# A decoder layer on one core: eighty TensorE transposes replaced by a layout exchange through DRAM

## The chip, the cores and the metric

The kernel runs on one core of a Trainium2 chip. A core has a matrix engine (TensorE, PE in the profile), a vector engine (DVE), a scalar engine (ACT), a general engine (POOL, hardly used here) and sixteen DMA engines that move data between DRAM, the on-chip memory (SBUF) and the accumulators (PSUM). DMA transfers are issued from queues; this kernel uses those of SP (weight loads) and of ACT (everything small). The metric is the device time of one execution in microseconds (us), median of several runs.

## The reference

```
h = rmsnorm(x, norm1_g)
z = h @ w_in                                  # 2048 -> 12824 columns
o_A, o_B, o_C, o_D = fox(z), conv(z), gla(z), pool(z)     # four mixers, 512 wide each
y = sum_n sigmoid(z_gate[n] + gate_b[n]) * (o_n @ w_branch[n])
x = x + y @ w_out
h2 = rmsnorm(x, norm2_g)
u = causal_dwconv(h2 @ ffn_up, ffn_dw, ffn_db);  a, v = split(u)
out = x + (silu(a) * v) @ ffn_down
```

Shapes: 256 tokens, width 2048, FFN width 5632 (a and v each), all float32.

## The kernel before

**Products.** Every product has 256 tokens on the output side, in two tiles of 128, and a quarter of 512 columns. The contraction runs over blocks of 128 rows. To keep float32 accuracy each operand is split into a high part in a reduced form and a rest: activations `xh`, `xl`, weights `wh`, `wl`. The generator `units` takes two contraction blocks at a time: SP loads raw weights `wr` (four blocks, 1 MB, three buffers), ACT casts them to `wh` (line 200), DVE subtracts to get `wl` (line 202); `wh` and `wl` have three buffers each. `product` then runs, for such a unit, eight matmuls with `wh` (lines 218 and 219) and four with `wl` (line 224). There are 545 units, nearly all of this size.

**Order.** Each engine works off its instructions in the order of the program. After a unit's matmuls `step` is called: it runs functions that were put down with `after(n, engine, f)` for this step, and those are placed on the engine behind the cast (A) or the subtraction (V) that was issued last. Because units are emitted three ahead of what TensorE does, what stands behind a cast stands ahead of the next one. Mixer work is emitted in small pieces between units by `pump`.

**Transposes.** An operand of a product must have its contraction rows on the partitions, while a result has tokens there. So results that become operands are turned. Before the change TensorE does it with 128x128 transposes against an identity into `pt`, eight for 256 tokens by 512 columns: `transposed_to` for the gate product of the convolution, the pooling input and the GLA queries and keys; `transposed` for the four quarters of y (line 268); a loop over the four quarters of the residual x (line 893). ACT and DVE copy or split `pt` afterwards.

**The FFN's exchange.** In the FFN the same turn is done without TensorE, in `half`. ACT puts the scaled result into `pu`, arranged by 32-row quarters. Four DMA transfers on ACT's queue (`mem<-pu`, 128 KB each, line 924) write it to a scratch tensor in DRAM, one fetch (`pw<-mem`, 512 KB, line 931) reads it back with quarters of rows and columns exchanged, and DVE turns each 32x32 block (STREAM_TRANSPOSE, line 937). The fetch comes six steps later, the turn nine. `pu` and `pw` have two buffers.

**Phases around the change.** First the convolution's two products and the pooling input; then gates and `branch` for each mixer, in the order 3, 1, 2, 0. In `branch(0)` each quarter of y is final: DVE multiplies the product by its gate (line 386), adds to y (387), and the quarter is transposed to `ah`, `al`. Then `w_out` takes four quarters of columns over y's four quarters of rows; each result is added to x (885), transposed, scaled into `h2h`, `h2l`, and squared for the norm (900). Then come FFN pairs.

Of the kernel before, what the change touches and what calls it, by code (L numbers as in the profile page):

```python
# [98 lines left out]
def layer(ctx, tc, a):  # L99
# [85 lines left out]
    def units(src, c0, n, sizes, loads, rows):  # L185

        k0 = have = 0
        loads = list(loads)
        for ks in sizes:
            if k0 == have:  # L190
                m = loads.pop(0)
                raw = wtile("wr", F32, m, n, LOAD, WR)
                nc.sync.dma_start(
                    out=raw,
                    in_=src[k0 * P : (k0 + m) * P, c0 : c0 + n].rearrange(rows, p=P),
                )
                base, have = k0, k0 + m
# [8 lines left out]
    def product(src, c0, n, stat, sizes=None, loads=None, tail=False, rows="(j p) n -> p j n"):  # L206

        nk = len(stat)
        acc = [accp.tile([P, 512], F32, name="acc") for _ in range(NT)]
        for k0, hi, lo in units(src, c0, n, sizes or [2] * (nk // 2), loads or [4] * (nk // 4), rows):  # L210
# [16 lines left out]
            step(1200.0)  # L227
        return acc

# [31 lines left out]
    def transposed(get, scales=None, tiles=None):  # L261

        hi, lo = tiles or act_tiles()
        for b in range(2):
            pt = tpp.tile([P, 2, S], F32, name="pt")
            for i in range(2):
                for t in range(NT):
                    T.transpose(pt[:, i, t * P : (t + 1) * P], get(t, 2 * b + i), ident)  # L268
            if scales is None:
                split_out(hi[:, 2 * b : 2 * b + 2], lo[:, 2 * b : 2 * b + 2], pt)  # L270
            else:
                for i in range(2):
                    split_out(hi[:, 2 * b + i], lo[:, 2 * b + i], pt[:, i], scales[2 * b + i])
        return hi, lo

# [3 lines left out]
    with ExitStack() as ph1:  # L279
        op_ = ph1.enter_context(tc.tile_pool(name="op", bufs=2))  # L280
        p1 = ph1.enter_context(tc.tile_pool(name="p1", bufs=1))
        gp = ph1.enter_context(tc.tile_pool(name="gp", bufs=5))
# [25 lines left out]
        def make_ssq(q):  # L308
            if q == 0:

                V.tensor_scalar(late, hT[3][1][:, 3, 0:1].bitcast(F32), 0.0, 0.0, ALU.max, ALU.min)
                A.activation(sqs, xts[q], AF.Square, bias=late)
            else:
                sq = gp.tile([P, 4, S], F32, name="gt")
                A.activation(sq, xts[q], AF.Square, bias=late)
                V.tensor_tensor(out=sqs, in0=sqs, in1=sq, op=ALU.add)
# [41 lines left out]
        def gates(n):  # L358
            out = []
            for d in range(4):  # L360
# [13 lines left out]
                out.append(g)  # L374
            return out

        def branch(n, g, oT, first=False, done=None):
            st = stationary([oT])
            for d in range(4):
                acc = product(w_branch[n], d * BW, BW, st)  # L380
                for t in range(NT):
# [3 lines left out]
                    else:  # L385
                        V.tensor_tensor(out=g[d][:, t], in0=acc[t], in1=g[d][:, t], op=ALU.mult)
                        V.tensor_tensor(out=yd, in0=yd, in1=g[d][:, t], op=ALU.add)
                if done is not None:
                    done(d)
# [85 lines left out]
        def logsig(pp, src, n, tag):  # L475

            e = pp.tile([P, n], F32, name=tag + "e")
# [5 lines left out]
        def gla_branch(pp, zc, gqT, gkT, tms, msk, wab, oT):  # L483
# [14 lines left out]
            e = logsig(pp, pl, 512, "gl")  # L498
# [8 lines left out]
            sr = pp.tile([P, NT, BW], F32, name="sr")  # L507
            A.activation(sr, zc[:, :, 528:1040], AF.Sigmoid)
            V.tensor_tensor(out=sr, in0=sr, in1=zc[:, :, 528:1040], op=ALU.mult)
            yield 1100  # L510
            go = pp.tile([P, NT, BW], F32, name="go")
# [117 lines left out]
        def fox_branch(pp, za, fb, sel, cb, msel, oT):  # L629
            rq = pp.tile([P, NT * 16], F32, name="fss")  # L630
            for t in range(NT):
                sq = pp.tile([P, 1024], F32, name="fsq")
# [32 lines left out]
            e = logsig(pp, lff, 16, "fl")  # L665
# [30 lines left out]
            fo = pp.tile([P, NT, BW], F32, name="fo")  # L696
# [69 lines left out]
        with tc.tile_pool(name="pDB", bufs=1) as pp:  # L766
# [9 lines left out]
            sg = gp.tile([P, NT, BW], F32, name="gt")  # L776
# [5 lines left out]
            later += [lambda q=q: make_ssq(q) for q in range(4)] + [make_rstd, gate_evac]  # L782
# [4 lines left out]
            nc.sync.dma_start(out=rc, in_=a["consts"][:, K_RC : K_RC + 64])  # L787
            for t in range(NT):
                V.scalar_tensor_tensor(
                    out=sg[:, t], in0=acca[t], scalar=rstd[:, t : t + 1], in1=sg[:, t],  # L790
                    op0=ALU.mult, op1=ALU.mult,
                )
            transposed_to(
                [lambda pt, b=b: A.copy(out=up[:, 2 * b : 2 * b + 2, CK - 1 :], in_=pt) for b in range(2)], sg
            )
            oB = o_tiles()
            later.append(lambda: bg.append(conv_branch(pp, up, oB)))
# [8 lines left out]
            zd = gp.tile([P, NT, BW], F32, name="gt")  # L806
            z_tok(zd, C_PZ, BW, BW)
            transposed_to(
                [lambda pt, b=b: A.copy(out=s0[:, 2 * b : 2 * b + 2, 16:], in_=pt) for b in range(2)], zd
            )  # L810
            oD = o_tiles()
            later.append(lambda: bg.insert(0, pool_branch(pp, pw, (s0, s1), oD)))
# [33 lines left out]
        with tc.tile_pool(name="pA", bufs=1) as pp:  # L846
# [5 lines left out]
            sst = pp.tile([P, 1024], F32, name="sst")  # L852
# [10 lines left out]
            g = gates(0)  # L863
            drain()
            yT = []
            branch(
                0, g, oA,
                done=lambda d: yT.append(
                    transposed(lambda t, i: y[:, t, (4 * d + i) * P : (4 * d + i + 1) * P])
                ),  # L870
            )
# [7 lines left out]
    h2S = []  # L879
    ss2 = p2.tile([P, NT, 4], F32, name="ss2")  # L880
    for d in range(4):
# [6 lines left out]
        for b in range(2):  # L888
            pt = tpp.tile([P, 2, S], F32, name="pt")
            for i in range(2):  # L890
                c = 4 * d + 2 * b + i
                for t in range(NT):
                    T.transpose(pt[:, i, t * P : (t + 1) * P], x2[:, t, c * P : (c + 1) * P], ident)  # L893
            for i in range(2):
                c = 4 * d + 2 * b + i
                split_out(hi[:, 2 * b + i], lo[:, 2 * b + i], pt[:, i], vec("n2", c))
        h2S += stationary([(hi, lo)])
        for t in range(NT):
# [3 lines left out]
            )  # L902
    s2 = p2.tile([P, NT], F32, name="s2s")
# [4 lines left out]
    up_ = ctx.enter_context(tc.tile_pool(name="fu", bufs=2))  # L908
    scr = ctx.enter_context(tc.tile_pool(name="scr", bufs=2, space=bass.MemoryType.DRAM))

    def half(pair, is_v, u):

        n = (NPAIR if is_v else 0) + pair
        acc = product(ffn_up, n * BW, BW, h2S)

        pu = up_.tile([P, 4, NT, P], F32, name="pu")
        for t in range(NT):
            A.activation(
                pu[:, :, t], acc[t].rearrange("p (q x) -> p q x", q=4), AF.Identity, scale=rstd2[:, t : t + 1]
            )  # L920

        mem = scr.tile([P, 4 * NT * P], F32, name="mem")
        for q in range(4):
            A.dma_start(
                out=mem[32 * q : 32 * q + 32].rearrange("r (k c) -> k r c", k=4),
# [110 lines left out]
```

## Time and profile before

| what | value |
|---|---|
| median of 3 runs | 1509.15 us (1508.7 to 1509.52) |
| profiled execution | 1508.69 us, span 1506.9 us |
| TensorE busy | 1501.5 us of the span |
| DVE busy | 997.9 us |
| ACT busy | 768.6 us |
| granted TensorE clock | 1.0 |

The span is the time from the first to the last instruction of the profiled execution; 1.8 us lie around it. An engine counts as busy only while it runs an instruction that computes; issuing a DMA counts as idle.

### The profile page before, as it was taken

How to read it: one execution, taken by the hardware profiler on the slowest of the kernel's cores; microseconds unless marked ns; L12 is line 12 of the kernel's file. 1: busy time of each engine (PE TensorE's matmuls, PEld its weight loads, DVE VectorE, ACT ScalarE, POOL GpSimd, SP SyncE). 2: the span in 40 equal slices, each digit the busy share in tenths (PEclk: the TensorE clock that was granted, in tenths of full speed). 3: DMA queues.
4: the chain of work that ended last, by engine and by line, in shares of the span. 5: the costliest groups of instructions: out<-in, count | busy, mean ns of one | idle time of the engine just before them, and what ended most of it. 6: DMA issues, size and time to landing. Idle time of an engine off the chain costs nothing.

```text
span 1506.9 us, 18227 instructions
## 1 busy us (share of the span) xinstructions
PE 1501.5 (100%) x7020; PEld 1259.6 (84%) x7020; DVE 997.9 (66%) x1272; ACT 768.6 (51%) x961; POOL 0.2 (0%) x4
## 2 busy tenths in 40 slices
PE   9999999999999999999999999999999999999998
PEld 8888889878998888888888888888888888888887
DVE  7799755666655656557555777764677745775775
ACT  7444365636456543444554655544555445544553
POOL 0000000000000000000000000000000000000000
PEclk9999999999999999999999999999999999999999
DMA  9656656545665466656556767765776657666774
GB/s 305 218 194 204 206 164 207 183 162 174 183 194 164 150 207 196 201 195 225 194 171 221 244 231 252 246 198 188 253 247 228 214 192 246 224 221 222 237 238 140
DMA packets 165450, 314.19 MB, mean 209 GB/s; under 512 B 6369, under 2 KB 32882, under 8 KB 164978
## 3 DMA queue, kind: packets, MB, share of 16 engines
q1 hardware_dynamic: 149680, 288.22, 58.3%
q10 hardware_dynamic: 15682, 24.81, 4.7%
q8 instruction: 55, 0.90, 0.2%
q14 instruction: 33, 0.27, 0.1%
HBM read 299.37 MB, written 13.63 MB: 208 GB/s over the span
## 4 chain that ended last, share of the span: by engine, by line
PE 99%; DMA 0%; DVE 0%; issue 0%; ACT 0%; ACTq 0%
PE acc L218 32%; PE acc L219 32%; PE acc L224 32%; PE mx L560 1%; DMA wr<-in_w_in 0%; PE mx L752 0%; PE mx L130 0%; PE mx L711 0%; PE pt L893 0%; PE pt L268 0%; PE mx L744 0%; PE pt L351 0%; PE mx L528 0%; PE mx L584 0%; PE mx L613 0%; PE mx L527 0%
## 5 line engine op out<-in xcount | busy, mean ns | idle before, releaser
L202 DVE TENSOR_TENSOR wl<-wr,wh 128x1024 fp32r<-128x1024 f32 (+4 forms) x545 | 646.4, 1189 | 422.6 <-ACT wh L200 420.1
L200 ACT CAST wh<-wr 128x1024 fp32r<-128x1024 f32 (+4 forms) x545 | 555.7, 1024 | 628.4 <-PE acc L219 548.7
L218 PE MATMUL acc<-wh,ah 128*128 128x512 f32 (+3 forms) x1344 | 514.2, 383 | 0.3 <-ACT wh L200 0.3
L219 PE MATMUL acc<-wh,al 128*128 128x512 f32 (+3 forms) x1344 | 511.9, 381 | 0.0
L224 PE MATMUL acc<-wl,ah 128*128 128x512 f32 (+3 forms) x1344 | 347.3, 380 | 0.0
L218 PEld LDWEIGHTS acc<-wh,ah 128*128 128x128 f32 x1344 | 252.7, 188 | 45.1 <-ACT wh L200 1.4
L219 PEld LDWEIGHTS acc<-wh,al 128*128 128x128 f32 x1344 | 252.7, 188 | 43.0 <-issue 0.6
L224 PEld LDWEIGHTS acc<-wl,ah 128*128 128x128 f32 x1344 | 249.1, 188 | 43.8
L219 PE MATMUL acc<-wh,h2l 128*128 128x512 f32 x704 | 274.0, 389 | 0.0
L218 PE MATMUL acc<-wh,h2h 128*128 128x512 f32 x704 | 273.9, 389 | 0.0
L224 PE MATMUL acc<-wl,h2h 128*128 128x512 f32 x704 | 188.2, 389 | 0.0
L219 PEld LDWEIGHTS acc<-wh,h2l 128*128 128x128 f32 x704 | 132.2, 188 | 27.4
L224 PEld LDWEIGHTS acc<-wl,h2h 128*128 128x128 f32 x704 | 132.1, 188 | 27.4
L218 PEld LDWEIGHTS acc<-wh,h2h 128*128 128x128 f32 x704 | 132.1, 188 | 27.3
L441 DVE SCALAR_TENSOR_TENSOR cacc<-up,vecT,cacc 128x256 f32<-128x256 f32 x120 | 51.0, 484 | 0.0
L218 PE MATMUL acc<-wh,oh 128*128 128x512 f32 x128 | 49.8, 389 | 0.0
L219 PE MATMUL acc<-wh,ol 128*128 128x512 f32 x128 | 49.8, 389 | 0.0
L937 DVE STREAM_TRANSPOSE zt<-pw 128x512 f32<-128x512 f32 x44 | 45.7, 1079 | 0.0
L953 ACT ACTIVATE ua<-ua 128x256 f32<-128x256 f32 x44 | 18.2, 414 | 48.8 <-issue 20.8
L948 DVE SCALAR_TENSOR_TENSOR uv<-zt,vecT,uv 128x255 f32<-128x255 f32 x88 | 41.7, 481 | 1.3
L948 DVE SCALAR_TENSOR_TENSOR ua<-zt,vecT,ua 128x255 f32<-128x255 f32 x88 | 41.3, 480 | 0.8
L983 DVE TENSOR_TENSOR x<-acc,x 128x512 f32<-128x512 f32 x40 | 25.8, 685 | 15.6 <-PE acc L224 15.6
(228 smaller groups left out, 641.5 us busy)
## 6 DMA issues: line engine op xcount, KB each, us to landing
wr<-in_ffn_up SPq DMA_DIRECT2D x88, 1024.0 KB
wr<-in_w_in SPq DMA_DIRECT2D x76, 1024.0 KB
wr<-in_ffn_down SPq DMA_DIRECT2D x44, 1024.0 KB
wr<-in_w_branch SPq DMA_DIRECT2D x16, 1024.0 KB
wr<-in_w_out SPq DMA_DIRECT2D x16, 1024.0 KB
wr<-in_w_in SPq DMA_DIRECT2D x16, 772.0 KB
mem<-pu ACTq DMA_DIRECT2D x88, 128.0 KB
pw<-mem ACTq DMA_DIRECT2D x22, 512.0 KB
```

The costliest lines, as they stand in the source:

```text
L200: mark["A"] = A.copy(out=hi, in_=part)
L202: mark["V"] = V.tensor_tensor(out=lo, in0=part, in1=hi.bitcast(F32), op=ALU.subtract)
L218: T.matmul(o, xh[:, s], hi[:, j], start=(k0 + j == 0), stop=False)
L219: T.matmul(o, xl[:, s], hi[:, j], start=False, stop=False)
L224: T.matmul(acc[t][:, :n], xh[:, s], lo[:, j], start=False, stop=(k0 + j == nk - 1))
L441: V.scalar_tensor_tensor(out=acc[:, c], in0=up[:, c, j : j + S], scalar=vec("cw", 4 * j + c), in1=acc[:, c], op0=ALU.mult, op1=ALU.add,)
L560: T.matmul(pss[h][:, q * P : (q + 1) * P], l_, r_, start=True, stop=True)
L937: V.transpose(out=zt[:, :, t * P : (t + 1) * P].rearrange("p j (k i) -> p j k i", k=4), in_=pw[:, :, t].rearrange("p k (i j) -> p j k i", ...
L948: V.scalar_tensor_tensor(out=u[:, c, sh:], in0=zt[:, c, : S - sh], scalar=vec("fw", tap * 88 + ch), in1=u[:, c, sh:], op0=ALU.mult, op1=AL ...
L953: A.activation(u[:, c], u[:, c], AF.Silu)
L983: V.tensor_tensor(out=x2[:, t, ds], in0=acc[t], in1=x2[:, t, ds], op=ALU.add)
```

## The change

The exchange of the FFN becomes a class `Exchange` that takes a tile pool, and is used for ten more turns: the gate product, the pooling input, the four quarters of y and the four of x. Their 80 TensorE transposes go; eight remain of those in `transposed_to` (GLA queries and keys). The turn reads contiguous blocks of four instead of a stride of four, so the weight columns of the FFN convolution and the rows of `ffn_down` change their order. The new pool `xq`, for the early exchanges and y, has one buffer; x uses the FFN's pool `fu`, which has two.

At two phase borders products run two at a time (`twin`): the first two quarters of `w_out` run over contraction blocks 0 to 7 each, then over 8 to 15, and the first FFN pair is cut at block 12. The gates of branch 0 are made in two halves, each followed by its two branch quarters.

```diff
+    def twin(src, c0s, n, stat, cut, done):
+        nk = len(stat)
+        accs = [acc_tiles() for _ in c0s]
+        for k0, k1 in ((0, cut), (cut, nk)):
+            for i, c0 in enumerate(c0s):
+                sizes = [2] * ((k1 - k0) // 2)
+                multiply(accs[i], n, stat, units(src, c0, n, sizes, [4] * ((k1 - k0) // 4), k0))
+                if k1 == nk:
+                    done(i, accs[i])
...
+    class Exchange:
+        def __init__(self, pool):
+            self.pool = pool
+            self.pu = pool.tile([P, 4, NT, 4, 32], F32, name="pu")
+        def put(self, t):
+            return self.pu[:, :, t].rearrange("p q j i -> p j q i")
+        def send(self):
+            self.mem = scr.tile([P, 4 * NT * P], F32, name="mem")
+            for q in range(4):
+                A.dma_start(
+                    out=self.mem[32 * q : 32 * q + 32].rearrange("r (k c) -> k r c", k=4),
+                    in_=self.pu[:, q].rearrange("p t j i -> p (t j i)"),
+                )
+        def fetch(self):
+            self.pw = self.pool.tile([P, 4, NT, 4, 32], F32, name="pw")
+            A.dma_start(out=self.pw.rearrange("p k t j i -> p (k t j i)"), in_=self.mem)
+        def turn(self, out):
+            for t in range(NT):
+                V.transpose(
+                    out=out[:, :, t * P : (t + 1) * P].rearrange("p j (k i) -> p j k i", k=4),
+                    in_=self.pw[:, :, t].rearrange("p k j i -> p j k i"),
+                )
+        def go(self, n_fetch, n_turn, out):
+            self.send()
+            after(n_fetch, "A", self.fetch)
+            after(n_turn, "V", lambda: self.turn(out))
+
+    xq = ctx.enter_context(tc.tile_pool(name="xq", bufs=1))
...
-                        V.tensor_tensor(out=yd, in0=yd, in1=g[d][:, t], op=ALU.add)
+                        if done is None:
+                            V.tensor_tensor(out=yd, in0=yd, in1=g[d][:, t], op=ALU.add)
+                        else:
+                            if t == 0:
+                                ex = Exchange(xq)
+                            V.tensor_tensor(out=ex.put(t), in0=cols(yd), in1=cols(g[d][:, t]), op=ALU.add)
...
-            g = gates(0)
+            g = gates(0, (0, 1))
             drain()
             yT = []
-            branch(
-                0, g, oA,
-                done=lambda d: yT.append(
-                    transposed(lambda t, i: y[:, t, (4 * d + i) * P : (4 * d + i + 1) * P])
-                ),
-            )
+            def y_done(ex):
+                hi, lo = act_tiles()
+                yT.append((hi, lo))
+                yt = xq.tile([P, 4, S], F32, name="yt")
+                ex.go(6, 8, yt)
+                after(9, "V", lambda: split_out(hi, lo, yt))
+            branch(0, g, oA, done=y_done)
+            branch(0, gates(0, (2, 3)), oA, done=y_done)
...
     nc.sync.dma_start(out=x2, in_=a["x"][0].rearrange("(t p) d -> p t d", p=P))
     yS = stationary(yT)
-    h2S = []
+    up_ = ctx.enter_context(tc.tile_pool(name="fu", bufs=2))
+    h2 = []
     ss2 = p2.tile([P, NT, 4], F32, name="ss2")
-    for d in range(4):
-        acc = product(w_out, d * BW, BW, yS)
+
+    def out_done(d, acc):
+        ex = Exchange(up_)
         for t in range(NT):
             xd = x2[:, t, d * BW : (d + 1) * BW]
             V.tensor_tensor(out=xd, in0=acc[t], in1=xd, op=ALU.add)
+            A.copy(out=ex.put(t), in_=cols(xd))
         hi = hp.tile([P, 4, S], F32R, name="h2h", tag="h2h")
         lo = hp.tile([P, 4, S], F32R, name="h2l", tag="h2l")
-        for b in range(2):
-            pt = tpp.tile([P, 2, S], F32, name="pt")
-            for i in range(2):
-                c = 4 * d + 2 * b + i
-                for t in range(NT):
-                    T.transpose(pt[:, i, t * P : (t + 1) * P], x2[:, t, c * P : (c + 1) * P], ident)
-            for i in range(2):
-                c = 4 * d + 2 * b + i
-                split_out(hi[:, 2 * b + i], lo[:, 2 * b + i], pt[:, i], vec("n2", c))
-        h2S += stationary([(hi, lo)])
+        h2.append((hi, lo))
+        xt = up_.tile([P, 4, S], F32, name="zt", bufs=1)
+        ex.go(6, 8, xt)
+        def scaled():
+            for i in range(4):
+                split_out(hi[:, i], lo[:, i], xt[:, i], vec("n2", 4 * d + i))
+        after(9, "V", scaled)
         for t in range(NT):
             sq = p2.tile([P, BW], F32, name="sq2", bufs=2)
             A.activation(
                 sq, x2[:, t, d * BW : (d + 1) * BW], AF.Square, accum_out=ss2[:, t, d : d + 1]
             )
+
+    twin(w_out, (0, BW), BW, yS, 8, out_done)
+    for d in (2, 3):
+        out_done(d, product(w_out, d * BW, BW, yS))
```

Not shown: the same replacement for the gate product and the pooling input (`ex.go(6, 8, ...)` each, and one more multiplication of the gate on ACT), the FFN's use of the class with (6, 9), the twin call for the first FFN pair with cut 12, and tiles that are reused to make room (`gp` has four buffers instead of five).

**DVE at the last two quarters of y (d2 and d3 of branch 0), before.** `gt<-acc,gt` is the gate multiply, `y<-y,gt` the final sum, `al<-pt,ah` the split of a transposed half.

```order
L386 TENSOR_TENSOR gt<-acc,gt 128x512 x2
L387 TENSOR_TENSOR y<-y,gt 128x512 x2
L202 TENSOR_TENSOR wl<-wr,wh 128x1024
L248 TENSOR_TENSOR al<-pt,ah 128x512 x2
L202 TENSOR_TENSOR wl<-wr,wh 128x1024
```

The same engine and place after the change; `pu<-y,gt` is the sum, written into the exchange's layout, and `yt<-pw` the turns.

```order
L434 TENSOR_TENSOR gt<-acc,gt 128x512 x2
L440 TENSOR_TENSOR pu<-y,gt 128x4x4x32 x2
L202 TENSOR_TENSOR wl<-wr,wh 128x1024 x2
L434 TENSOR_TENSOR gt<-acc,gt 128x512 x2
L440 TENSOR_TENSOR pu<-y,gt 128x4x4x32 x2
L202 TENSOR_TENSOR wl<-wr,wh 128x1024 x4
L280 STREAM_TRANSPOSE yt<-pw 128x4x128 x2
L202 TENSOR_TENSOR wl<-wr,wh 128x1024
L310 TENSOR_TENSOR al<-yt,ah 128x1024
L202 TENSOR_TENSOR wl<-wr,wh 128x1024
L280 STREAM_TRANSPOSE yt<-pw 128x4x128 x2
```

The split stood one subtraction behind the sum; now four subtractions and the turns lie between the last put and the first split, and the second put stands two subtractions behind the first.

**ACT at the same place, after the change.** `mem<-pu` are the four sends of a quarter, `pw<-mem` the fetch; before, this engine had here only casts and pairs of `L247 CAST ah<-pt 128x512`.

```order
L200 CAST wh<-wr 128x1024 x3
L268 DMA mem<-pu 4x32x256 x4
L200 CAST wh<-wr 128x1024 x2
L268 DMA mem<-pu 4x32x256 x4
L275 DMA pw<-mem 128x1024
L200 CAST wh<-wr 128x1024 x3
L275 DMA pw<-mem 128x1024
L309 CAST ah<-yt 128x1024
L200 CAST wh<-wr 128x1024 x2
L309 CAST ah<-yt 128x1024
```

The fetch of the first of the two quarters now stands directly behind the sends of the second.

**ACT at the last quarter of x, before.** `sq` are the squares, `h2h<-pt` scaled casts of transposed quarters, `x2r` the square root for the norm.

```order
L250 ACTIVATE h2h<-pt,vecT 128x256 x2
L200 CAST wh<-wr 128x1024
L250 ACTIVATE h2h<-pt,vecT 128x256 x2
L235 ACT_TABLE_LOAD
L235 ACTIVATE x2r<-x2v 128x2
L200 CAST wh<-wr 128x1024 x7
```

The same place after the change:

```order
L941 COPY pu<-x_5559 128x4x4x32
L955 ACTIVATE sq_6221,ss_5564<-x_5559 128x512
L941 COPY pu<-x_5559 128x4x4x32
L955 ACTIVATE sq_6223,ss_5564<-x_5559 128x512
L268 DMA mem<-pu 4x32x256 x4
L297 ACT_TABLE_LOAD
L297 ACTIVATE x2r<-x2v 128x2
L200 CAST wh<-wr 128x1024 x3
L275 DMA pw<-mem 128x1024
L200 CAST wh<-wr 128x1024 x3
L312 ACTIVATE h2h<-zt,vecT 128x256 x4
```

Two copies and four sends came in ahead of the next cast; the scaled casts moved six casts back.

## Rows read from the trace of the kernel before

**Rows 1.** The profile page: span, busy time of each engine, chain of waits.

```profile
span 1506.9 us, 18227 instructions
...
PE 1501.5 (100%) x7020; PEld 1259.6 (84%) x7020; DVE 997.9 (66%) x1272; ACT 768.6 (51%) x961; POOL 0.2 (0%) x4
...
PE 99%; DMA 0%; DVE 0%; issue 0%; ACT 0%; ACTq 0%
```

**Rows 2.** Timeline of TensorE, starts of units: start us, duration, line, operation.

```profile
665.17 0.39 PE L218 MATMUL acc<-wh,ah 128*128 128x512 f32 x1
...
667.89 0.39 PE L218 MATMUL acc<-wh,oh 128*128 128x512 f32 x1
...
673.34 0.39 PE L218 MATMUL acc<-wh,oh 128*128 128x512 f32 x1
...
677.03 0.39 PE L218 MATMUL acc<-wh,oh 128*128 128x512 f32 x1
...
715.36 0.39 PE L218 MATMUL acc<-wh,ah 128*128 128x512 f32 x1
...
719.10 0.39 PE L218 MATMUL acc<-wh,ah 128*128 128x512 f32 x1
```

**Rows 3.** Groups on TensorE: busy us, mean ns of one, idle time before.

```profile
L893 PE MATMUL pt<-ident,x 128*128 128x128 f32 x32 | 5.0, 280 | 0.0
L268 PE MATMUL pt<-ident,y 128*128 128x128 f32 x32 | 5.0, 279 | 0.0
...
L351 PE MATMUL pt<-ident,gt 128*128 128x128 f32 x24 | 3.6, 272 | 0.0
```

**Rows 4.** Timeline of ACT and DVE in a steady stretch, idle before in brackets.

```profile
659.03 1.05 ACT L200 CAST wh<-wr 128x1024 fp32r<-128x1024 f32 x1 [1.67 <-PE acc L219]
...
660.12 1.23 DVE L202 TENSOR_TENSOR wl<-wr,wh 128x1024 fp32r<-128x1024 f32 x1 [1.50 <-ACT wh L200]
```

**Rows 5.** Timeline of ACT in the FFN: put, sends, casts, fetch.

```profile
808.05 2.35 ACTq L924 DMA_DIRECT2D mem<-pu  x4
810.50 2.00 ACT L200 CAST wh<-wr 128x1024 fp32r<-128x1024 f32 x2 [2.48 <-issue]
...
816.35 0.35 ACTq L931 DMA_DIRECT2D pw<-mem  x1
```

**Rows 6.** DMA activity from 852 to 861 us in forty slices: tenths busy, GB/s.

```profile
DMA  9999999624222222222222222229974999999999
GB/s 382 437 419 410 391 400 401 228 50 109 91 91 77 68 82 87 91 96 100 82 77 77 96 91 96 96 96 191 205 100 155 264 341 337 355 419 423 423 369 400
```

**Rows 7.** DMA queues from 1317.4 to 1322.6 us, from the fetch's issue on.

```profile
q10 hardware_dynamic: 143, 0.52, 25.7%
```

**Rows 8.** Groups by form on DVE and ACT: busy us, mean ns of one.

```profile
L937 DVE STREAM_TRANSPOSE zt<-pw 128x512 f32<-128x512 f32 x44 | 45.7, 1079 | 0.0
...
L386 DVE TENSOR_TENSOR gt<-acc,gt 128x512 f32<-128x512 f32 x24 | 15.5, 686 | 7.4 <-PE acc L224 7.4
...
L250 ACT ACTIVATE h2h<-pt,vecT 128x256 fp32r<-128x256 f32 x16 | 6.7, 469 | 0.0
...
L235 ACT ACT_TABLE_LOAD x4 | 5.1, 1283 | 0.1
L900 ACT ACTIVATE sq<-x 128x512 f32<-128x512 f32 x8 | 5.0, 625 | 1.4 <-DVE x L885 1.4
```

**Rows 9.** Timeline of ACT's queue: two of three loads of constants.

```profile
201.43 0.35 ACTq L819 DMA_DIRECT2D gx<-in_consts  x1
...
202.29 0.53 ACTq L826 DMA_DIRECT2D wab<-in_gla_ba  x1
```

**Rows 10.** DMA packets from 203 to 204.9 us, all of ACT's queue.

```profile
DMA packets 77, 0.63 MB, mean 332 GB/s; under 512 B 0, under 2 KB 0, under 8 KB 0
```

**Rows 11.** Timeline of SP's queue: the load of the residual x.

```profile
696.04 0.37 SPq L877 DMA_DIRECT2D x<-in_x  x1
```

**Rows 12.** DMA queues from 697 to 703 us; the last column is the share.

```profile
q1 hardware_dynamic: 300, 2.14, 99.5%
```

More of the change, by code (lines that the diff above doesn't have):

```diff
@@ L183, in wtile, with units @@
         return w[:, : ks * BW].rearrange("p (j n) -> p j n", j=ks)[:, :, :n]
-    def units(src, c0, n, sizes, loads, rows):
-        k0 = have = 0
+    def units(src, c0, n, sizes, loads, k0=0):
+        have = k0
         loads = list(loads)
@@ L204, in units, with multiply @@
             k0 += ks
-    def product(src, c0, n, stat, sizes=None, loads=None, tail=False, rows="(j p) n -> p j n"):
+    def multiply(acc, n, stat, groups, tail=False):
         nk = len(stat)
-        acc = [accp.tile([P, 512], F32, name="acc") for _ in range(NT)]
-        for k0, hi, lo in units(src, c0, n, sizes or [2] * (nk // 2), loads or [4] * (nk // 4), rows):
+        for k0, hi, lo in groups:
             ks = hi.shape[1]
@@ L227, in product, with acc_tiles, cols @@
             step(1200.0)
-        return acc
+    def acc_tiles():
+        return [accp.tile([P, 512], F32, name="acc") for _ in range(NT)]
+    def product(src, c0, n, stat, sizes=None, loads=None, tail=False):
+        nk = len(stat)
+        acc = acc_tiles()
+        multiply(acc, n, stat, units(src, c0, n, sizes or [2] * (nk // 2), loads or [4] * (nk // 4)), tail)
+        return acc
+    def twin(src, c0s, n, stat, cut, done):
+        nk = len(stat)
+        accs = [acc_tiles() for _ in c0s]
[5 more added lines that the diff above has]
+                    done(i, accs[i])
+    scr = ctx.enter_context(tc.tile_pool(name="scr", bufs=2, space=bass.MemoryType.DRAM))
+    def cols(ap):
+        return ap.rearrange("p (j q i) -> p j q i", q=4, i=32)
+    class Exchange:
[25 more added lines that the diff above has]
+    xq = ctx.enter_context(tc.tile_pool(name="xq", bufs=1))
     def rsqrt(pool, ssq, n, scale, tag):
@@ L356, in transposed_to, with gates @@
             later.extend([None, lambda: half(0), lambda: half(1)])
-        def gates(n):
-            out = []
-            for d in range(4):
+        def gates(n, ds=range(4)):
+            out = {}
+            for d in ds:
                 bias = gp.tile([P, BW], F32, name="gb", tag="gb", bufs=3)
@@ L378, in branch @@
             st = stationary([oT])
-            for d in range(4):
+            for d in g:
                 acc = product(w_branch[n], d * BW, BW, st)
@@ L805, in layer @@
             V.memset(pool_tmp[:, 0:16], 0.0)
[L806 to L810, printed above, removed]
+            ex = Exchange(xq)
+            acc = product(w_in, C_PZ, BW, hS)
+            for t in range(NT):
+                A.activation(ex.put(t), cols(acc[t]), AF.Identity, scale=rstd[:, t : t + 1])
+            ex.go(6, 8, s0[:, :, 16:])
             oD = o_tiles()
-            later.append(lambda: bg.insert(0, pool_branch(pp, pw, (s0, s1), oD)))
+            after(8, "V", lambda: bg.insert(0, pool_branch(pp, pw, (s0, s1), oD)))
             g = gates(3)
@@ L905, in layer, with half @@
     rstd2 = rsqrt(p2, s2, NT, 1.0 / D, "x2")
[L908 to L911 removed]
+    def half(pair, is_v, u, acc):
         n = (NPAIR if is_v else 0) + pair
[L914 to L916 removed]
+        ex = Exchange(up_)
         for t in range(NT):
[L918 to L925, printed above, removed]
[L926 to L940 removed]
+            A.activation(ex.put(t), cols(acc[t]), AF.Identity, scale=rstd2[:, t : t + 1])
+        zt = up_.tile([P, 4, S], F32, name="zt", bufs=1)
         def conv(c):
@@ L953, in conv @@
                 A.activation(u[:, c], u[:, c], AF.Silu)
-        after(6, "A", fetch)
-        after(9, "V", turn)
+        ex.go(6, 9, zt)
         for c in range(4):
@@ L963, in pair_up @@
         hi, lo = act_tiles()
-        half(pair, False, ua)
-        half(pair, True, uv)
+        us = (ua, uv)
+        c0s = [(is_v * NPAIR + pair) * BW for is_v in range(2)]
+        if pair == 0:
+            twin(ffn_up, c0s, BW, h2S, 12, lambda i, acc: half(pair, i, us[i], acc))
+        else:
+            for i in range(2):
+                half(pair, i, us[i], product(ffn_up, c0s[i], BW, h2S))
         def glu():
@@ L980, in down @@
             ds = slice(d * BW, (d + 1) * BW)
-            acc = product(w, d * BW, BW, st, tail=last and d == 3, rows="(p j) n -> p j n")
+            acc = product(w, d * BW, BW, st, tail=last and d == 3)
             for t in range(NT):
```

79 lines of the change are left out of this document (25 added, 54 removed).

## Prediction

> **What bounds the kernel now.** The page comes first: TensorE is busy 1501.5 of 1506.9 us, and the chain of waits is 99% PE [rows 1]. So the time falls only by what TensorE no longer does, and rises by any wait put in its way. Next the timeline of TensorE: a "unit" (8 products with wh, then 4 with wl) starts at 665.17 and the next at 667.89, 2.72 us on. At a border with transposes a unit lasts longer: 673.34 to 677.03 in the stage of y, 715.36 to 719.10 in that of x [rows 2].
>
> The groups of TensorE give what those transposes cost by their number: 32 for y, 32 for x, 24 in the helper of the first phase [rows 3]. Their busy times (5.0, 5.0, 3.6) overlap other matmuls; the unit lengths tell the truth.
>
> Then the engines that feed TensorE. Each unit needs a cast on ACT (1.05 us) and a subtraction on DVE (1.22 us). In a steady stretch ACT starts the cast at 659.03 and ends it near 660.1, DVE subtracts from 660.12 to 661.35 [rows 4], and TensorE starts that unit at 665.17, since three buffers stand between them. So wh is 5.1 us ahead. wl is first read after 8 of the 12 products, 8/12 x 2.72 = 1.8 us into the unit, so it is 5.6 us ahead. **This lead is what any new work queued ahead of a cast or a subtraction may eat; what exceeds it stalls TensorE.**
>
> **What the change removes.** 80 transposes in ten groups of 8: four quarters of y, four of x, the gate product and the pooling input. A unit with a group of 8 costs 3.69 - 2.72 = 0.97 us more in y, 3.74 - 2.72 = 1.02 in x [rows 2]. The two early groups have no row of their own here; at the same 0.97 each, 10 groups give **-9.9 us**. Nothing hides this: TensorE has no other idle time.
>
> **What it adds.** Each group becomes an exchange: a put into pu, four sends to DRAM, a fetch into pw, two turns on DVE. No engine work lands on TensorE, so each costs nothing until it overruns the lead. The FFN already does this, and gives prices. ACT issues four sends from 808.05 in 2.35 us, and its fetch, which waits for all four, issues at 816.35: 8.3 us until pu is free and the data is in DRAM [rows 5]. The sends run at some 90 GB/s in the tail of the window, at two tenths of the DMA engines [rows 6]. The fetch's 0.52 MB are through 5.2 us after its issue, with loads beside them [rows 7]; I take 5. A turn pair is 2 x 1.08 us, the gate multiply and the put 0.69 us for each half [rows 8].
>
> **The y borders.** Let 0 be the start of w_branch quarter d3 (or d1), units 2.72 apart; d2 has just ended. DVE multiplies and puts d2 until 3.1, ACT ends the third cast ahead at 3.1 and sends. xq has one buffer, so pu is free at 3.1 + 8.3 = 11.4. The product of d3 ends at 5.4 and its put could run from 6.8, but must wait: it ends at 11.4 + 1.4 = 12.8. Queued behind it on DVE is the subtraction of the unit that starts at 10.9: it ends at 14.0, TensorE wants it at 10.9 + 1.8 = 12.7. Stall 1.3 us, at both borders. Without the wait this put costs nothing.
>
> Next, the sends of d3 issue from 12.8 and the fetch of d2 right behind them at 15.4, on the same queue. If the fetch is independent it lands at 20.4. If its packets go behind the sends', it lands when these have (12.8 + 8.3 = 21.1) plus 1.3 for its 0.52 MB at some 400 GB/s [rows 6], at 22.4. The trace favours the latter: a load of constants was issued at 201.43, and two small ones behind it by 202.29 + 0.53 [rows 9], yet from 203 to 204.9 the queue moved 77 packets, none under 8 KB [rows 10]. [...] The turn and the subtraction behind it (2.1 + 1.2) must end by 21.8 + 1.3 + 1.8 = 24.9, so the fetch must land by 21.6: 0 or 0.8 us of stall. First border: 1.3 + 0.8 = **2.1**.
>
> At the second border the residual x (2.1 MB) is loaded on the SP queue. Its place is memory that y held, so it waits for the put of d3 and issues at the same 12.8 as the sends. Before, it was issued at 696.04 [rows 11] and ran alone, 2.14 MB in 6.0 us at 99.5% of all sixteen engines [rows 12]. How it shares engines with the sends no row shows. Lower bound: no harm, 0.8 us. Upper bound: its 6.0 us go ahead of the sends, the fetch lands at 28.4, stall 6.8. The nearest rows lie on both sides (weight loads just before and after sends leave them their 90 GB/s [rows 6]; the load of x takes every engine [rows 12]), so I take the middle, **3.8**.
>
> Two more steps follow here alone, because w_out reads d2 and d3 soon: the cast of ah queues ahead of wh (0.3 us), and the fetch of d3 waits for the turn of d2, pw being single. From the end of that turn 5 + 2.1 + 1.2 = 8.3 us pass to the subtraction that TensorE wants after 1.2 + 5.4 = 6.7: 1.6, less the 0.3 already lost, 1.3. Second border: 1.3 + 3.8 + 0.3 + 1.3 = **6.7**. y together 8.8, bounds 3.1 (no order, no harm) to 11.8.
>
> **The x borders.** Here pu and pw are double. Per quarter ACT has two copies (as long as a square, 0.63), two squares and the sends (2.35), after two adds on DVE (1.4) [rows 8, 5]. From the end of the product: sends from 3.5, ended 5.8, the cast behind them done 6.9; TensorE wants it at 8.2. So d0 is free. Its fetch holds ACT until 3.5 + 8.3 = 11.8; a cast later, at 13.2, ACT can take up d1, its twin, which ended at 10.9. Sends from 15.8, the cast behind them done at 19.2, wanted at 10.9 + 8.2 = 19.1: the lead is used up. The fetch of d1 holds ACT until 15.8 + 8.3 = 24.1; then come four scaled casts (4 x 0.47), three casts, and four scaled casts that wait for the turns, to 33.6. DVE, behind the same turns, adds d2 (ended 32.6) only from 36; ACT's sends end at 41.8, the next cast at 42.8, wanted at 40.8. That is 1.9 late if nothing gives way, 0 from a clean start; halfway, 0.9. d3 has a table load and a root (1.5) between its sends and the next cast: 6.9 + 1.5 = 8.4 for 8.2, and DVE's adds come up to 2.5 late again, as one subtraction and four splits (1.2 + 4 x 0.48) stand ahead of them: 0.2 to 2.7. d2's backlog is certain to last in part, so I take 2.1. Sum **3.0**, bounds 0.2 and 4.7.
>
> **Small edits.** The early exchanges: the turns come eight units after the put and the engines have over 1.7 us of lead left; the conv and pooling start later, but are fillers whose results are wanted many units on. 0, at most 1. The two-at-a-time FFN pair moves two evacuations closer: 0 to 1.5, I take 0, since its leads come out at 1.3 and 1.9. The other row order of ffn_down and of the weight columns, the reused tiles: same bytes and counts, 0.
>
> **Sum** against the profiled execution: 1508.69 - 9.9 + 8.8 + 3.0 = **1510.6 us**. That execution lies 0.46 under the median of the runs, inside their spread.
>
> **Rivals.**
> - *The load of x goes wholly ahead of the sends* (slower). Place: the second y border. Price: S = 6.8 instead of 3.8, so 1513.6; it decides once that stall passes 4.9 us. For it: the load takes every engine [rows 12]. Against: sends lost little next to weight loads [rows 6]. [...]
> - *The fetch does not wait for the sends behind which it is queued*, and x does no harm. Both borders 1.3, the second 0.5 for pw: y 3.1, so 1508.69 - 9.9 + 3.1 + 3.0 = 1504.9. For it: sends take two tenths of the engines, most are free [rows 6]. Against: [rows 9, 10].
> - *The leads absorb nearly everything*: puts are not held because sends land sooner than the fetch's issue suggests (8.3 is when ACT came to it), and x starts clean. Then 1499 to 1501. For it: ACT waits 1.67 us for TensorE in every steady unit [rows 4]. Against: four sends alone already hold an FFN cast back by 2.48 us [rows 5], and one pu cannot be refilled before it is read.
>
> **Numbers.** A measurement of this kernel tells 0.2% (3.0 us) from no change. Forecast 0.35, rival one 0.25, two 0.25, three 0.15. Faster: three, and half of two, with a little of the forecast's lower side (0.30). Slower: most of rival one and of the forecast's upper side (0.30). Same: the rest, 0.40. The range leaves out three and what exceeds the upper bounds: 1503.5 to 1515.5.
>
> **What would show it.** Right: no transposes at the borders, TensorE gaps of about 1 us two units after each y border ended by DVE; the put of d1 and d3 waiting on mem<-pu for some 4 us; turns of d2 waiting on the fetch; the cast after x's sends ending the waits of TensorE. Wrong: units at 2.72 us straight through the borders (rival three), or one gap of over 5 us at the load of x (rival one). What would make it wrong altogether is a stall where I put none, in the twin pair of the FFN or in the early phase.

## The result and the profile after

The changed kernel takes 1525.49 us (median of 4 runs, 1524.68 to 1528.14) against 1509.04 before: ratio 1.0112, interval 1.0094 to 1.0129. It is slower by 16.5 us, where 1.9 us were forecast. Its profiled execution took 1525.28 us.

The page of the changed kernel:

```profile
span 1523.5 us, 18152 instructions
...
PE 1500.5 (98%) x6940; PEld 1256.7 (82%) x6940; DVE 992.6 (65%) x1288; ACT 765.4 (50%) x963; POOL 0.2 (0%) x4
...
PEclk9999999999999999998999999999999999999999
...
PE 86%; DVE 5%; DMA 4%; ACT 2%; issue 2%; ACTq 1%; SPq 0%; DVEq 0%
```

TensorE runs 80 products fewer than in [rows 1] (6940 against 7020), but it is no longer nearly the whole chain of waits (86% against 99%), and one slice in the middle has less than nine tenths of the granted clock. So the saving is there, and more than that was lost to waits. The waits of all engines in groups (engine and line that waited, what released it: us in all, times, longest) name them:

```profile
ACT wh L200 <- DMA wr<-in_w_out: 16.3, 1, 16.3
...
DVE pu L440 <- DMA mem<-pu: 13.0, 2, 6.5
...
DVE yt L280 <- DMA pw<-mem: 10.2, 2, 6.5
PE acc L217 <- ACT wh L200: 9.8, 5, 4.7
...
PE acc L223 <- DVE wl L202: 7.1, 3, 2.8
```

The two middle lines are the y borders: DVE waits 13.0 us in two places for the sends to free pu, and 10.2 us for fetches. The last two are what TensorE paid itself.

Where it was paid is read from single units, which take 2.72 us undisturbed [rows 2]. Each window here runs from one unit's start to the next one's, with the busy time of each engine, then the granted clock:

```profile
core 0: us, PE busy (x) PEld busy (x) DVE busy (x) ACT busy (x) POOL busy (x), PEclk, DMA share, GB/s
64.39:68.53 4.14, 2.89 (x13) 2.07 (x11) 0.02 (x1) 1.09 (x2) 0.00 (x0) 1.00 0.42 142
640.79:647.08 6.29, 3.48 (x14) 2.49 (x12) 3.56 (x4) 0.00 (x0) 0.00 (x0) 0.92 0.16 52
647.08:650.93 3.85, 3.85 (x14) 3.08 (x12) 2.36 (x2) 2.73 (x3) 0.00 (x0) 0.69 0.87 259
656.37:660.81 4.44, 3.00 (x13) 2.18 (x12) 3.06 (x4) 1.73 (x2) 0.00 (x0) 1.00 0.45 148
701.62:707.45 5.83, 3.02 (x14) 2.18 (x13) 3.53 (x4) 0.00 (x0) 0.00 (x0) 1.00 0.33 84
707.45:716.62 9.17, 4.49 (x14) 3.24 (x12) 0.06 (x2) 1.10 (x2) 0.00 (x0) 0.69 0.89 339
716.62:721.55 4.93, 4.93 (x13) 3.92 (x14) 2.34 (x2) 1.84 (x2) 0.00 (x0) 0.54 0.62 209
800.77:805.59 4.82, 2.88 (x14) 2.07 (x12) 1.15 (x8) 3.11 (x7) 0.00 (x0) 1.00 0.59 222
805.59:810.03 4.44, 4.44 (x12) 3.54 (x13) 3.48 (x4) 2.58 (x3) 0.00 (x0) 0.62 0.61 195
869.89:874.46 4.57, 2.89 (x14) 2.07 (x12) 3.76 (x9) 2.50 (x5) 0.00 (x0) 1.00 0.66 242
```

Length less 2.72: 1.4 us early (64.39); 3.6, 1.1 and 1.7 at the first y border (640.79 to 660.81); 3.1, 6.5 and 2.2 at the second (701.62 to 721.55); 2.1 and 1.7 at the last quarter of x (800.77 to 810.03); 1.9 in the first FFN pair (869.89). That is 25.3 us. Against it stand the 9.9 us removed: +15.4 of the measured 16.6 between the two profiled executions. Ten units explain nearly all.

In the units from 647.08, 707.45, 716.62 and 805.59 the granted clock is 0.54 to 0.69: it stands at 0.50 for a part of each, from 646.1 to 649.4 us for instance and from 714.3 to 721.1, and at 1.00 from 649.5 to 652. In the window ahead of each of them TensorE stood still for 2.8, 2.8, 4.7 and 1.9 us (length less PE busy). Behind the windows at 656.37 and 869.89, in which it stood still for 1.4 and 1.7 us, the clock stayed at 1.00.

How the first y border goes, on DVE:

```profile
635.32 1.29 DVE L434 TENSOR_TENSOR gt<-acc,gt 128x512 f32<-128x512 f32 x2 [0.68 <-PE acc L223]
643.08 1.29 DVE L440 TENSOR_TENSOR pu<-y,gt 128x512 f32<-128x512 f32 x2 [6.47 <-DMA mem<-pu]
644.29 2.35 DVE L202 TENSOR_TENSOR wl<-wr,wh 128x1024 fp32r<-128x1024 f32 x2
...
657.32 1.31 DVE L280 STREAM_TRANSPOSE yt<-pw 128x512 f32<-128x512 f32 x2 [6.53 <-DMA pw<-mem]
```

The sends of the first quarter began at 632.40. The put of the second waits 6.47 us for them, until 643.08, 10.7 us after that start, and the two subtractions behind it end too late: TensorE stands still for 2.8 us. Then the turn waits 6.53 us for its fetch, and TensorE 1.4 us for the subtraction behind the turn.

The second border, on ACT and on SP's queue:

```profile
693.24 2.27 ACTq L268 DMA_DIRECT2D mem<-pu  x4
...
705.25 7.45 ACTq L268 DMA_DIRECT2D mem<-pu  x4
712.79 2.63 ACTq L275 DMA_DIRECT2D pw<-mem  x1
715.52 2.94 ACT L200 CAST wh<-wr 128x1024 fp32r<-128x1024 f32 x3 [16.27 <-DMA wr<-in_w_out]
```

```profile
705.29 0.37 SPq L930 DMA_DIRECT2D x<-in_x  x1
```

The sends of d2 issue in 2.27 us, those of d3 in 7.45, and the fetch behind them in 2.63: the load of x was issued at the same time, 705.29. ACT can cast nothing until 715.52, and TensorE, done with the unit that started at 707.45, waits 4.7 us until 716.62 for the first cast. (The page puts ACT's 16.27 us down to a weight load; in 10.1 of them the engine issued.)

The first four sends of the second border in the view of the DMA engines (forty slices of 693.2 to 703.4 us, tenths busy; then packets, MB and share of the sixteen engines for each queue; q1 is SP's, q10 ACT's):

```profile
DMA  9998741222222994769999999874333332222222
...
q1 hardware_dynamic: 746, 1.47, 41.0%
q10 hardware_dynamic: 527, 0.52, 17.7%
```

Alone, they keep two to three tenths of the engines busy, as in [rows 6]. A weight load comes in between and fills the rest. At the end both queues share what little is still busy; from 700.5 to 703 us:

```profile
q1 hardware_dynamic: 95, 0.19, 19.8%
q10 hardware_dynamic: 82, 0.08, 9.6%
```

Together that is 29% of sixteen engines, 4.7 engines' worth (an estimate from the shares), and the sends last nearly the whole window. Where ACT's queue is the only one that moves anything, its share is 27.4%, or 4.4 engines' worth, from 718.4 to 719.7 us, and 27.1% from 811 to 813 us in the kernel before. The slowest dimension of such a send is 4 on its DRAM side and 128 on pu's; whether the low share comes from these shapes is what the first run below tries.

### The profile page after: what moved, and what is told of

Its sections match the earlier page's. It is cut to its first block, busy times and chain, and to the rows that moved or that the text cites. A ratio compares the mean times of both kernels' runs of the same rounds, so it can differ in the third digit from the quotient of the medians.

```text
span 1523.5 us, 18152 instructions
## 1 busy us (share of the span) xinstructions
PE 1500.5 (98%) x6940; PEld 1256.7 (82%) x6940; DVE 992.6 (65%) x1288; ACT 765.4 (50%) x963; POOL 0.2 (0%) x4
## 4 chain that ended last, share of the span: by engine, by line
PE 86%; DVE 5%; DMA 4%; ACT 2%; issue 2%; ACTq 1%; SPq 0%; DVEq 0%
PE acc L217 28%; PE acc L218 28%; PE acc L223 28%; DMA mem<-pu 3%; DVE cacc L494 2%; DVE wl L202 2%; ACT wh L200 1%; ACTq L268 1%; DMA pw<-mem 1%; PE mx L612 1%; DMA wr<-in_w_out 1%; PE mx L804 0%; DMA wr<-in_w_in 0%; DVE y L432 0%; PE mx L763 0%
## 5 line engine op out<-in xcount | busy, mean ns | idle before, releaser
L218 PEld LDWEIGHTS acc<-wh,h2l 128*128 128x128 f32 x704 | 132.6, 188 | 27.4
L986 ACT ACTIVATE ua<-ua 128x256 f32<-128x256 f32 x44 | 18.2, 413 | 43.0 <-issue 20.7
L1020 DVE TENSOR_TENSOR x<-acc,x 128x512 f32<-128x512 f32 x40 | 25.9, 686 | 16.6 <-PE acc L223 16.6
L280 DVE STREAM_TRANSPOSE zt<-pw 128x512 f32<-128x512 f32 x52 | 33.8, 688 | 3.4 <-DMA pw<-mem 3.4
```

Of the source, the lines that this page charges most:

```text
L218: T.matmul(o, xl[:, s], hi[:, j], start=False, stop=False)
L280: V.transpose(out=out[:, :, t * P : (t + 1) * P].rearrange("p j (k i) -> p j k i", k=4), in_=self.pw[:, :, t].rearrange("p k j i -> p j k i"),
L986: A.activation(u[:, c], u[:, c], AF.Silu)
L1020: V.tensor_tensor(out=x2[:, t, ds], in0=acc[t], in1=x2[:, t, ds], op=ALU.add)
```

## The experiments

**Wide sends.** Each send now takes 32 partitions of pu and writes all their row quarters; bytes, pieces of 1 KB and number of sends are the same.

```diff
-            for q in range(4):
+            for k in range(4):
                 A.dma_start(
-                    out=self.mem[32 * q : 32 * q + 32].rearrange("r (k c) -> k r c", k=4),
-                    in_=self.pu[:, q].rearrange("p t j i -> p (t j i)"),
+                    out=self.mem.rearrange("(q r) (k c) -> r q k c", q=4, k=4)[:, :, k],
+                    in_=self.pu[32 * k : 32 * k + 32].rearrange("p q t j i -> p q (t j i)"),
                 )
```

> Edit: each of the four sends takes 32 partitions of pu and writes their four row quarters, so that its slowest dimension is 32 instead of 4; same bytes, same 1 KB pieces, same number of sends (also in the FFN). Theory A (sends run on few DMA engines, hold pu for 10.7 us, and this sets both y stalls): sends are through in about 5 us instead of 8 to 11, the first y border falls from 6.4 us of loss to under 1, the second from 11.8 to 2 to 5 (the load of x still collides), the early loss of 1.6 goes; time about 1508, between 1504 and 1513. Theory B (the new work queued on ACT and DVE is what overruns the lead, whatever the sends take): little changes, 1520 or more.

Measured: 1499.47 us (1499.07 to 1499.7), ratio to before 0.9936 (0.9921 to 0.9951): 9.6 us faster than before, 26.0 faster than the changed kernel. The page and TensorE's whole list of waits:

```profile
span 1497.3 us, 18163 instructions
...
PE 1491.8 (100%) x6940; PEld 1251.7 (84%) x6940; DVE 995.0 (66%) x1288; ACT 771.9 (52%) x963; POOL 0.2 (0%) x4
...
PEclk9999999999999999999999999999999999999999
```

```profile
PE mx L130 <- DVE ones L125: 1.0, 1, 1.0
```

The view lists no wait of TensorE after its start. TensorE's busy time fell from 1501.5 us [rows 1] to 1491.8, about as much as the kernel's time. DMA engines during the sends of the first x quarter (723.1 to 726.6 us):

```profile
DMA  9999999779999998999899888899999998961000
...
q10 hardware_dynamic: 576, 0.52, 60.6%
```

The same 0.52 MB are through within these 3.5 us, at seven to nine tenths, weights beside them included, and a send of 128 KB landed 2.4 us after its issue (median of the four). With slowest dimensions of 32 and 32 instead of 4 and 128, ACT's queue has 60.6% of sixteen engines, 9.7 engines' worth (an estimate from the share), where it had 27% alone. So the shape of a send sets how much of the engines it keeps busy here; why it does, no run shows. And DVE at the first y border:

```profile
633.15 1.29 DVE L434 TENSOR_TENSOR gt<-acc,gt 128x512 f32<-128x512 f32 x2 [0.68 <-PE acc L223]
634.35 1.22 DVE L202 TENSOR_TENSOR wl<-wr,wh 128x1024 fp32r<-128x1024 f32 x1
635.48 1.29 DVE L440 TENSOR_TENSOR pu<-y,gt 128x512 f32<-128x512 f32 x2
636.69 1.22 DVE L202 TENSOR_TENSOR wl<-wr,wh 128x1024 fp32r<-128x1024 f32 x1
```

The put at 635.48 follows its multiply with a subtraction between and waits for nothing; the sends had begun at 630.23, so pu was free within 5.3 us. Theory A holds, more fully than expected; B falls: the same work is queued on ACT and DVE, and the leads hold it. At the second border, beside the load of x, the units lost 0.3 us.

**Wide sends without the change.** The same edit in the FFN of the kernel before.

```diff
-        for q in range(4):
+        for k in range(4):
             A.dma_start(
-                out=mem[32 * q : 32 * q + 32].rearrange("r (k c) -> k r c", k=4),
-                in_=pu[:, q].rearrange("p t x -> p (t x)"),
+                out=mem.rearrange("(q r) (k c) -> r q k c", q=4, k=4)[:, :, k],
+                in_=pu[32 * k : 32 * k + 32].rearrange("p q t x -> p q (t x)"),
             )
```

> Edit: the kernel before, with the wide sends in its FFN and nothing of the change. Control for the 1499.5 us of the changed kernel with wide sends. If those come from the removed transposes alone, wide sends do nothing here, since TensorE does not wait in the FFN: 1509.0, within 1 us. If wide sends gain by themselves, 1505 or less.

Measured: 1508.75 us (10 runs) against 1508.85, ratio 0.9999 (0.9990 to 1.0008). The wide sends are worth nothing where TensorE does not wait; so the 9.6 us are not theirs, and the fall of TensorE's busy time says that they are those of the removed transposes.

**Wide sends for y alone.**

```diff
-        def __init__(self, pool):
-            self.pool = pool
+        def __init__(self, pool, is_y=False):
+            self.pool, self.is_y = pool, is_y
...
+            if self.pool is xq and self.is_y:
+                for k in range(4):
...
+            else:
+                for q in range(4):
...
-                                ex = Exchange(xq)
+                                ex = Exchange(xq, True)
```

> Edit: wide sends for the four quarters of y only; the early exchanges, x and the FFN keep the narrow ones. If the places add up, the 17.8 us of the y borders go and the 1.6 (early), 4.1 (x) and 2.0 us (first FFN pair) stay: 1507.5 (1506 to 1509.5). If x and the FFN stall only because y made them late, 1501 or less.

Measured: 1507.26 us (median of 10, 1503.08 to 1509.94).

**y by transposes again.** All else stays changed, with narrow sends.

```diff
...
-                        if done is None:
-                            V.tensor_tensor(out=yd, in0=yd, in1=g[d][:, t], op=ALU.add)
-                        else:
-                            if t == 0:
-                                ex = Exchange(xq)
-                            V.tensor_tensor(out=ex.put(t), in0=cols(yd), in1=cols(g[d][:, t]), op=ALU.add)
+                        V.tensor_tensor(out=yd, in0=yd, in1=g[d][:, t], op=ALU.add)
...
+            def y_done(d):
+                yT.append(transposed(lambda t, i: y[:, t, (4 * d + i) * P : (4 * d + i + 1) * P]))
```

> Edit: the four quarters of y are transposed by TensorE again, as before the change; everything else of the change stays, with the narrow sends. If the losses read from the trace of the changed kernel add up (6.4 and 11.8 us at the y borders against 3.9 us of transposes saved there), undoing y gives back 14.3: 1511 (1509 to 1513). If the losses are hidden in one another, so that the x stage would wait instead, the time stays above 1517.

Measured: 1511.42 us (median of 10, 1506.99 to 1512.9). Both medians come out within 0.5 us of what the single units gave, though the ten runs of each lie 6 to 7 us apart. The places add up: y's borders cost 1525.5 - 1507.3 = 18.2 us, the early phase, x and the first FFN pair 1507.3 - 1499.5 = 7.8 together.

**A second pu for y.** The put of each y quarter goes to a free buffer of the gate pool.

```diff
-        def __init__(self, pool):
+        def __init__(self, pool, pu=None):
...
-            self.pu = pool.tile([P, 4, NT, 4, 32], F32, name="pu")
+            self.pu = pu if pu is not None else pool.tile([P, 4, NT, 4, 32], F32, name="pu")
...
-                                ex = Exchange(xq)
+                                ex = Exchange(xq, gp.tile([P, 4, NT, 4, 32], F32, name="gt"))
```

> Edit: y's pu is taken from the gate pool, whose four buffers are not all in use there, so that the put of d1 and d3 waits for nothing; pw stays single. Theory A1 (the single pu is the cause at both borders): the stalls of 3 us behind the put go, with the low clock after them; first border 6.4 to about 2, second 11.8 to about 7; time near 1516 (1513 to 1519). Theory A2 (the order in ACT's queue is the cause: the fetch still waits behind two quarters of sends): the stall moves to the turn, two to four units later, and the time falls by less than 4 us, to 1522 or more.

Measured: 1514.35 us (1511.61 to 1518.22), 11.1 less than the changed kernel. The waits on pu are gone; what is left at the borders comes to 2.2 and 5.2 us, read from its units as above, instead of 6.4 and 11.8. A1 holds: with narrow sends the single buffer carried more than half of what y's borders cost.

**The load of x later.**

```diff
-                nc.sync.dma_start(
+                mark["S"] = nc.sync.dma_start(
...
-    nc.sync.dma_start(out=x2, in_=a["x"][0].rearrange("(t p) d -> p t d", p=P))
+    def load_x2():
+        nc.sync.dma_start(out=x2, in_=a["x"][0].rearrange("(t p) d -> p t d", p=P))
+
+    after(12, "S", load_x2)
```

> Edit: the load of the residual x is issued after the weight load for the eleventh and twelfth unit of w_out instead of after the fourth load. Theory X (the load of x starves the second border's sends and holds ACT in their issue, which took 7.5 us instead of 2.3): the second border becomes like the first, 11.8 to about 6.4 us of loss, four sends issue in 2.3 us again; time near 1520 (1518 to 1522). Theory not X (the second border is worse for its early reader w_out): the time stays within 2 us of 1525.5.

Measured: 1521.95 us (1520.84 to 1523.19), 3.5 less. In the profiled executions 0.7 us of the gain lies in the early phase, which the edit does not touch. ACT issues its sends in 2.26 us again:

```profile
703.68 2.26 ACTq L268 DMA_DIRECT2D mem<-pu  x4
706.06 0.46 ACTq L275 DMA_DIRECT2D pw<-mem  x1
...
717.32 0.33 ACTq L275 DMA_DIRECT2D pw<-mem  x1
```

```profile
702.36 1.29 DVE L440 TENSOR_TENSOR pu<-y,gt 128x512 f32<-128x512 f32 x2 [6.41 <-DMA mem<-pu]
...
725.04 1.30 DVE L280 STREAM_TRANSPOSE yt<-pw 128x512 f32<-128x512 f32 x2 [3.91 <-DMA pw<-mem]
```

But the fetch of d3, issued at 717.32, now comes behind the load of x, issued at 710.54 on SP's queue, and its turn starts only at 725.04, 7.7 us after the issue. By its units the second border still loses 11.0 us instead of 11.8. The time lies in theory X's range of 1518 to 1522, but not for its reason: X was right on ACT's issue and wrong on the price, since the next transfer is late now; that the moved load holds it up is inferred from these times.

**TensorE kept busy in its waits.**

```diff
+    count = [0]
+    FILL = {(232, "lo"): 12, (252, "lo"): 12, (254, "hi"): 20, (285, "hi"): 8}
+
+    def busy_work(n):
+        if n:
+            mx = mxp.tile([P, 512], F32, name="mx")
+            for _ in range(n):
+                T.matmul(mx[:, :P], ones, ones, start=True, stop=True)
...
+            busy_work(FILL.get((count[0], "hi"), 0))
...
+                busy_work(FILL.get((count[0], "lo"), 0))
```

> Edit: at the four longest waits (units 232, 252, 254, 285) TensorE gets 12, 12, 20 and 8 idle products of 128 columns of ones ahead of the product that waits; nothing else changes. Theory C (the granted clock falls because TensorE idles for 2 us and more, and that costs on top of the waits): the clock stays at 1.0 behind the waits, the slow products (0.427 us each instead of 0.227) go, the waits stay as long; gain 4 to 7 us, near 1520. Theory not C (the clock falls for another reason, or the slow products are hidden in later waits): within 2 us of 1525.5, or slower by the added products.

Measured: 1525.51 us (median of 4, 1522.01 to 1528.43), against 1525.49 for the changed kernel. Four of its units:

```profile
641.40:647.20 5.80, 5.69 (x37) 5.01 (x36) 3.52 (x4) 0.00 (x0) 0.00 (x0) 1.00 0.14 48
655.38:661.94 6.56, 3.00 (x13) 2.17 (x12) 3.06 (x4) 1.73 (x2) 0.00 (x0) 1.00 0.52 179
708.54:717.99 9.45, 7.36 (x54) 6.69 (x52) 0.09 (x2) 1.10 (x2) 0.00 (x0) 1.00 0.85 331
717.99:720.82 2.83, 2.83 (x13) 2.36 (x14) 2.34 (x2) 1.85 (x2) 0.00 (x0) 1.00 0.59 220
```

The clock stays at 1.0 and the unit at 717.99 takes 2.83 us instead of 4.93. Yet the unit at 655.38 takes 6.56 where it took 4.44: what the first border saved in clock it waits for at the turn. By its units, the first border loses 6.9 us (6.4 before the edit), the second 11.6 (11.8), of which 9.9 lie in its units from 702.76 to 720.82 and the rest in a new wait at its last turn, and x 3.6 (4.1). The early phase, which the edit does not touch, lost 0.9 more in this execution. Theory C is right on the clock and wrong on its price: most of what the clock gave back went into waits for the transfers, and with runs up to 6.4 us apart a gain of a few us in the median can't be told from none.

**One exchange more.** Wide sends, and GLA's queries and keys exchanged too.

```diff
...
-            zq = gp.tile([P, NT, BW], F32, name="gt")
-            z_tok(zq, C_GQ, BW, BW)
...
+            ex = Exchange(xq)
+            acc = product(w_in, C_GQ, BW, hS)
+            for t in range(NT):
+                A.activation(ex.put(t), cols(acc[t]), AF.Identity, scale=rstd[:, t : t + 1])
+            ex.go(6, 8, qk)
+            after(9, "A", lambda: A.activation(gqT, gqT, AF.Copy, scale=64**-0.5))
```

> Edit: wide sends, and the last eight transposes of the first phases (GLA queries and keys) made an exchange too. If a group of eight costs TensorE 0.98 us wherever it stands and an exchange with wide sends is hidden, 1.0 us less than 1499.5, 1498.5. If TensorE's time for them was hidden in a wait, or the exchange is late for the GLA work, 1499.5 or more.

Measured: 1497.52 us (5 runs, 1497.12 to 1497.98), ratio to before 0.9925 (0.9911 to 0.9938), the fastest version here: 11.3 us less than the kernel before, measured beside it (1508.85). The gain over wide sends alone is 1.9 us where 1.0 was expected, 1.7 with each against the kernel before that was measured beside it; the two traces show 1.0 between their first and last units, so the rest is not settled.

## Why the prediction was wrong

The direction was forecast as no change with 0.40 and slower with 0.30; the time lies 10 us above the range.

- **What the change removes: right.** 9.9 us were worked out; 9.6 were measured with wide sends, once nothing waits.
- **The step that failed: "8.3 us until pu is free", the price of the sends,** and with it the bounds. That figure was read where ACT came to the fetch in the FFN; there the sends ran almost alone from 810 to 813.5 us (27.2% of sixteen engines, SP's queue 0.3%). At the y borders it was 10.7 us twice, with weight loads beside the sends: from 632.4 to 643.1 us SP's queue has 40.0% of sixteen engines and ACT's 16.8%. The lead was used up already, so TensorE waited 2.8 us behind each put where 1.3 stood in the sum. At the first border the waiting unit lost 3.6 us, the next one 1.1 at the lower clock, and the turn 1.7 where 0.8 stood: 6.4 us instead of 2.1. For y as a whole 8.8 us were forecast, and wide sends for y alone gave back 18.2.
- **The second border: 11.8 us instead of 6.7.** The collision with the load of x was seen and given as rival one with at most 6.8 us at the turn. Missing was that ACT itself stands in the issue of sends (7.45 us instead of 2.35) and of the fetch (2.63), so that its casts come late: a wait of 4.7 us at once. That a fetch is held by the sends ahead of it on its queue was right for about a quarter of its pieces. It issued at 712.79; some 90 of its 128 pieces of 4 KB moved from 715.9 to 717.7 us (177 pieces of its queue, less 89 under 2 KB), and between 717.7 and 720.4 us nearly all pieces are 1 KB, the sends', or weights:

```profile
DMA packets 301, 0.32 MB, mean 120 GB/s; under 512 B 20, under 2 KB 273, under 8 KB 301
```

The rest moved after that, at least 32 of them between 720.4 and 722.6 us (90 pieces of its queue, less 58 under 2 KB), and the turn started at 722.66. TensorE did not wait at the turns of this border, where 3.8 and 1.3 us stood in the sum; its waits here are 2.8 us behind the put and the 4.7 for the cast.
- **x: 3.0 forecast, 0.3 and 2.1 in waits, plus 1.7 at the lower clock.** The mechanism at the last quarter, ACT's sends and table load ahead of a cast, was right: the cast behind them began at 804.51, and TensorE waited for it until 805.59. The clock was in no term.
- **The small edits were not free.** The gate product's four sends began at 52.96, while weights filled the engines (SP's queue 89.5% of sixteen from 52.96 to 56.24 us, ACT's 0.4%), and its fetch held ACT until 66.98; it cost 1.4 us:

```profile
52.96 3.28 ACTq L268 DMA_DIRECT2D mem<-pu  x4
...
66.98 0.34 ACTq L275 DMA_DIRECT2D pw<-mem  x1
```

This loss is not steady: it was 0.8 us in the profiled execution with the later load of x and 3.8 in that with y by transposes, whose kernels are the same up to there, and this may be part of why the runs with narrow sends scatter. The first FFN pair, with two evacuations close together, cost 1.9, where 0 to 1.5 were allowed. Both losses go with wide sends.
- **Rivals.** Rival one was the nearest, and too small by the issue that holds ACT. The load of x did not go ahead as one block: from 709 to 711.5 us 25 pieces of the sends moved beside 126 of the load, of which some 32 stood on the engines of the sends if these are a quarter of the sixteen, as their share of 27% alone suggests, and all took equal parts (an estimate). But a piece of the load has 8 KB and one of the sends 1 KB, so it came to nearly the same: of the sends' 512 pieces at most 32 had moved at 712 us. Rival three, in which the leads absorb nearly everything (1499 to 1501), came true only with wide sends, which were no part of it. No rival said that the share of the engines that the sends keep busy decides. The rows had it: two tenths of the engines in [rows 6] were read as room left for others, not as the reason why the exchange is slow.

## What to carry to other kernels

Before work is moved from a busy engine to transfers, read how many DMA engines a transfer keeps busy: here four sends that kept two tenths of the engines busy held their buffer for 10.7 us beside weight loads, and the same bytes cut along another dimension held it for at most 5.3. Price a latency where it will be used, with the traffic that is there, not at the place where another engine happened to come to it. And a tile with a single buffer turns such a latency into a wait of the engine that fills it: 6.5 us of DVE's time at each y border here.

## What was not expected of the hardware

- The turn that reads contiguous runs of 32 elements is faster than the one that reads with a stride of four, 688 against 1079 ns [rows 8]:

```profile
L280 DVE STREAM_TRANSPOSE zt<-pw 128x512 f32<-128x512 f32 x52 | 33.8, 688 | 3.4 <-DMA pw<-mem 3.4
```

- Issuing a DMA can hold its engine for long: 7.45 us for four sends of 128 KB beside a load of 2 MB, 2.26 us at the same place with that load moved away. Why the issue is held no run here shows.
- The granted clock fell to 0.54 to 0.69 in the units behind the longest waits, and stayed at 1.0 when these were filled with products of ones; the median time was the same, 1525.51 against 1525.49 us.
